# Latent-head scores from high and low parts in five passes, with the value projection moved ahead of the convolved queries and keys

## The chip, the cores and the metric

The kernel runs on one core of a Trainium2 chip. The metric is device time in microseconds (us) of one execution, taken as the median of several runs; less is better. The engines have short names in the rows: PE is TensorE (its weight loads are PEld), DVE is VectorE, ACT is ScalarE, POOL is GpSimd, SP is SyncE, which issues most DMA transfers.

## The reference, cut to what matters

Two transformer blocks over 512 tokens of width 1024, in float32. The change lies in the first block's mixer, which has two groups of heads over one normalised input h:

```python
z = h @ w_in[l]
q_m, k_m, v_m, o_m, gates, c_q, c_kv, k_pe = jnp.split(z, splits, axis=-1)
qk = jax.nn.silu(conv_centred(jnp.concatenate([q_m, k_m], axis=-1), conv_w[l], conv_b[l]))   # 5 taps over time
q_m, k_m = qk[..., :M_QK_W], qk[..., M_QK_W:]
y_a = mlstm_group(q_m, k_m, v_m, o_m, gates, ...)          # four recurrent heads, both directions
y_b = mla_group(c_q, c_kv, k_pe, cos, sin, ...)            # four latent heads
x = x + jnp.concatenate([y_a, y_b], axis=-1) @ w_out[l]
...
# mla_group: q and k of 4 heads, 128 plain + 64 rotated columns
s = jnp.einsum('bhqd,bhkd->bhqk', q_blk, kh) * scale       # 192 columns
p = jax.nn.softmax(s, axis=-1)
return jnp.einsum('bhqk,bhkv->bhqv', p, vh)
```

## The kernel before

A tensor is kept as 128 partitions by free columns. Two kinds of float32 matmul occur. One reads plain float32 operands; the trace lists each of these as two instructions. The other reads operands of type F32R that were split into a high part (a copy on ACT, rounded to F32R) and a low part (the difference, `sub`, on DVE), and `mm3` (lines 129 to 132) adds three passes, high by high, high by low and low by high. Weights come in pages of 128x1024 and are split the same way by `page` (line 105 on ACT, line 86 on DVE).

The order on each engine is fixed when the program is built, by a scheduler that looks at when operands and rooms (tiles in a pool, PSUM banks) come free; at run time each engine goes through its list in order and waits where it must. PSUM has four banks tagged "acc" and four tagged "att".

The stages that matter, with times in the profiled span:

- Projections and latent heads, 41 to 112.8 us. Line 426 and before prepare the compressed queries and keys. `lat_in`, `lat_norm` and `lat_heads` (lines 470 to 539) make, for 4 token blocks by 2 (query and key), the heads, normalise and rotate them, and transpose them: line 531 transposes the plain part, line 533 copies it to `qT0`/`kT0`; line 536 transposes the rotated part, line 537 copies it to `qT1`/`kT1`. All four are plain float32. Between these, PE works off two projections that nothing waits for yet: first `pq` (4 pages `wf[0..3]`, the queries and keys of the recurrent heads, 96 passes), then `pts` (the values, `w_in_t[0..3]`, 96 passes).
- The convolution of each `pq` page (lines 591 to 616): on DVE one line 596 and four lines 599 (the five taps) into `cv`, the tanh on ACT (line 602), line 603 on DVE, then copies on ACT (608, 610) and differences on DVE (line 86) into `qk` and `ql`.
- Attention of the latent heads, 112.8 to 174.9 us: 16 steps (4 heads by 4 query blocks), staged over three steps. `lat_scores` (lines 551 to 567): two plain float32 matmuls into `psc` (line 556 over 128 rows, line 557 over 64 rows), maximum on DVE (559, 560), exponential on ACT (563), reciprocal and scaling on DVE (564, 565). `lat_turn`: four transposes `ppt` (572) and a copy `PT` (574). `lat_out`: four matmuls `pov` (582), then `ybh` on ACT (583) and `ybl` on DVE (line 86, `yb`).
- Recurrent heads, 174.9 to 232 us: `pM` (641) brings the running maxima into an "acc" bank, `pS` (652, 653) the scores into an "att" bank, DVE and ACT build the weights `E` (664 to 668), `pH` (679) multiplies them with the values `v1`. From 194.7 us the projection of the output gate (`pts`, `w_in_t[4..7]`) fills PE between them.

The scores before:

```python
        PE.matmul(ps, qT0[j][:, jj, q], kT0[j][:, jj, :], start=True, stop=False)
        PE.matmul(ps, qT1[pp, j, q], kT1[pp, j, :], start=False, stop=True)
```

Of the kernel before, what the change touches and what calls it, by code (L numbers as in the profile page):

```python
# [7 lines left out]
F32 = mybir.dt.float32  # L8
F32R = mybir.dt.float32r
# [5 lines left out]
OP = mybir.AluOpType  # L15
# [35 lines left out]
def body(ctx, tc, I, out):  # L51
# [334 lines left out]
    zero = mb.tile([P, T], F32, tag="PT", name="zero", bufs=2)[0:R]  # L386
    G.memset(zero, 0.0)
    Bc = mb.tile([P, T], F32, tag="PT", name="Bc", bufs=2)[0:R]
# [20 lines left out]
    for i in range(3):  # L409
# [5 lines left out]
        ch = lp.tile([P, T], F32R, name=f"ch{i}")  # L415
        cl = lp.tile([P, T], F32R, name=f"cl{i}")
# [21 lines left out]
    qT0 = [main.tile([P, 2, T], F32, tag="x", name="qT0", bufs=NT) for _ in range(2)]  # L438
    kT0 = [main.tile([P, 2, T], F32, tag="x", name="kT0", bufs=NT) for _ in range(2)]
    qT1 = mb.tile([P, 2, T], F32, name="qT1")  # L440
    kT1 = mb.tile([P, 2, T], F32, name="kT1")
# [83 lines left out]
    def lat_heads(tb, key):  # L525
        nope, rot = lat[tb, key]
        T0, T1 = (kT0, kT1) if key else (qT0, qT1)
# [4 lines left out]
        for j in range(2):  # L532
            S.activation(T0[j][:, :, t], pt[:, j * 256:(j + 1) * 256].rearrange("p (h t) -> p h t", h=2), AF.Copy)
# [3 lines left out]
        S.activation(T1[:, :, t], pt[:, 0:256].rearrange("p (h t) -> p h t", h=2), AF.Copy)  # L537
# [13 lines left out]
    def lat_scores(hd, qb):  # L551
# [4 lines left out]
        PE.matmul(ps, qT0[j][:, jj, q], kT0[j][:, jj, :], start=True, stop=False)  # L556
        PE.matmul(ps, qT1[pp, j, q], kT1[pp, j, :], start=False, stop=True)
# [10 lines left out]
    def lat_turn(hd, qb):  # L568
        pe_ = att[hd, qb]
        pt = bank("att", "ppt")  # L570
        for sb in range(NT):
            PE.transpose(pt[:, sb * P:(sb + 1) * P], pe_[:, sb * P:(sb + 1) * P], ident)
        PT = mb.tile([P, NT, P], F32, tag="PT", name="PT", bufs=2)
        S.activation(PT, pt.rearrange("p (s t) -> p s t", s=NT), AF.Copy)
        att[hd, qb] = PT

# [13 lines left out]

    qk = []
    for i in range(4):
        ps = bank("acc", "pq")
        ws_mm(ps, page(wf[i]), h, l)
        cv = mc.tile([P, T], F32, tag="cv", name="cv", bufs=2)
        V.tensor_scalar(cv, ps, convw[:, i, 2:3], convw[:, i, 5:6], op0=OP.mult, op1=OP.add)
        for j in (0, 1, 3, 4):
            a, b = max(0, 2 - j), min(T, T + 2 - j)
            V.scalar_tensor_tensor(cv[:, a:b], ps[:, a + j - 2:b + j - 2], convw[:, i, j:j + 1], cv[:, a:b],
                                   op0=OP.mult, op1=OP.add)  # L600
        th = mc.tile([P, T], F32, tag="th", name="th", bufs=1)
        S.activation(th, cv, AF.Tanh, scale=0.5)
        V.scalar_tensor_tensor(th, th, 1.0, cv, op0=OP.add, op1=OP.mult)
        if i < 2:
            ql = mv.tile([P, T], F32R, name=f"ql{i}")
        for m, (own, other) in enumerate(((up, dn_), (dn_, up))):
            a = mv.tile([P, T], F32R, name=f"qk{i}{m}")
            S.activation(a[own], th[own], AF.Copy)
            if i < 2:
                S.activation(a[other], th[own], AF.Copy)  # L610
                sub(V, ql[own], th[own], a[own])
                qk.append((a, ql))
            else:
                sub(V, a[other], th[own], a[own])
                qk.append(a)


# [5 lines left out]

    def ev_o(tb, ps):
        S.activation(og[:, tb], ps, AF.Tanh, scale=0.5)
        V.scalar_tensor_tensor(og[:, tb], og[:, tb], 1.0, gm_b, op0=OP.add, op1=OP.mult)

    ts_mm([I["w_in_t"][j] for j in range(4)], range(KT), h, l, ev_v)
    mb_close()
    mc_close()  # L630


    ma, ma_close = pool("rec")
    og = ma.tile([P, NT, 512], F32, name="og")
    rec = {}
# [790 lines left out]
```

## Time and profile before

| | us |
|---|---|
| median of 3 runs (2143.5 to 2150.49) | 2144.11 |
| the profiled execution | 2146.64 |
| its span in the trace | 2144.8 |
| PE busy | 2096.8 (98%) |
| DVE busy | 1544.4 (72%) |
| ACT busy | 857.7 (40%) |

The profiled execution is 2.5 us above the median and lies inside the runs; 1.8 us of it are outside the span. A busy share is a mean over stages with different limits, so the rows below are taken stage by stage. A timeline row gives the start, the duration, the engine, the line, the operation, the tile written and the tiles read, the shape, the count of merged instructions, and in brackets the idle time of the engine before it and who ended that. Durations of neighbouring instructions overlap; the distance from one start to the next is what an instruction costs its engine.

### The profile page before, as it was taken

To read this page: it belongs to the slowest core of one execution; us is meant where nothing else is said; L and a number is where in the kernel's file an instruction comes from. 1 tells how busy PE (TensorE), PEld (TensorE's weight loads), DVE (VectorE), ACT (ScalarE), POOL (GpSimd) and SP (SyncE) were. 2 spreads that over 40 slices of the span, in tenths; PEclk is the share of its full clock that TensorE was granted. 3 is DMA by queue.
4 is the path that set the end of the run, shared out by engine and by line. 5 is a ranking of instruction groups with operands and counts; after the bars stand their busy time and mean duration, and the time that the engine had idled before them with its cause. 6 is when DMAs were issued, how large, how long until landed. Compare 5 with 4: busy or idle time off the path is not lost.

```text
span 2144.8 us, 29733 instructions
## 1 busy us (share of the span) xinstructions
PE 2096.8 (98%) x10985; PEld 1812.1 (84%) x10985; DVE 1544.4 (72%) x3037; ACT 857.7 (40%) x1504; POOL 504.0 (23%) x387
## 2 busy tenths in 40 slices
PE   8999999999999999999999999999999999999987
PEld 7856888888888778888999998888989989898976
DVE  6846675556454663689879697788888888888765
ACT  5745354444234543311345544333333333333323
POOL 1200034445100000100000002354444444444420
PEclk9999999999999999999999999999999999999999
DMA  5200279999422213345898857899999999999873
GB/s 199 69 30 20 89 256 343 324 347 345 170 68 89 70 61 102 124 163 178 284 364 301 280 187 242 286 360 362 342 349 338 335 336 349 337 345 341 280 234 108
DMA packets 178113, 504.40 MB, mean 235 GB/s; under 512 B 15536, under 2 KB 73776, under 8 KB 171184
## 3 DMA queue, kind: packets, MB, share of 16 engines
q1 hardware_dynamic: 135344, 326.33, 45.4%
q0 software_dynamic: 42624, 176.18, 21.9%
q8 instruction: 86, 1.41, 0.3%
q14 instruction: 59, 0.48, 0.1%
HBM read 426.95 MB, written 75.50 MB: 234 GB/s over the span
## 4 chain that ended last, share of the span: by engine, by line
PE 87%; DMA 5%; issue 3%; DVE 3%; ACT 1%; POOL 1%; SPq 0%; POOLq 0%; DVEq 0%; ACTq 0%
PE pA L130 10%; PE pA L131 10%; PE pA L132 10%; PE po L131 7%; PE po L132 7%; PE po L130 7%; PE pO L131 3%; PE pO L132 3%; PE pO L130 3%; PE pts L132 2%; PE pts L130 2%; PE pts L131 2%; PE pGm L1143 2%; DMA gv<-peer_v,eidx 2%; DMA gu<-peer_u_rows,eidx 1%
## 5 line engine op out<-in xcount | busy, mean ns | idle before, releaser
L130 PE MATMUL pA<-xTh,Ah 128*128 128x384 f32 (+1 forms) x1256 | 433.8, 345 | 0.3 <-ACT ge L1162 0.3
L132 PE MATMUL pA<-xTh,Al 128*128 128x384 f32 (+1 forms) x1256 | 434.1, 346 | 0.0
L131 PE MATMUL pA<-xTl,Ah 128*128 128x384 f32 (+1 forms) x1256 | 433.9, 345 | 0.0
L105 ACT ACTIVATE Ah<-raw 128x1024 fp32r<-128x1024 f32 x197 | 208.9, 1061 | 377.5 <-PE pA L131 266.7
L86 DVE TENSOR_TENSOR Al<-raw,Ah 128x1024 fp32r<-128x1024 f32 x196 | 242.8, 1239 | 144.1 <-ACT Ah L105 139.9
L1229 POOL DMA_INDIRECT gu<-peer_u_rows,eidx x128 | 172.6, 1348 | 607.2 <-ACT Wh L1286 404.8
L131 PE MATMUL po<-Bl,Wh 128*128 128x512 f32 x750 | 294.6, 393 | 14.1 <-DVE Bl L86 14.1
L132 PE MATMUL po<-Bh,Wl 128*128 128x512 f32 x750 | 294.3, 392 | 0.0
L130 PE MATMUL po<-Bh,Wh 128*128 128x512 f32 x750 | 281.5, 390 | 0.0
L131 PEld LDWEIGHTS pA<-xTl,Ah 128*128 128x128 f32 x1256 | 235.8, 188 | 13.2
L130 PEld LDWEIGHTS pA<-xTh,Ah 128*128 128x128 f32 x1256 | 235.8, 188 | 13.1 <-ACT ge L1162 0.6
L132 PEld LDWEIGHTS pA<-xTh,Al 128*128 128x128 f32 x1256 | 235.8, 188 | 9.3
L1240 POOL DMA_INDIRECT gv<-peer_v,eidx x128 | 169.6, 1325 | 222.6 <-DVE x L1242 202.4
L86 DVE TENSOR_TENSOR Bl<-raw,Bh 128x1024 fp32r<-128x1024 f32 x157 | 200.7, 1279 | 22.0 <-ACT Bh L105 21.7
L1286 ACT ACTIVATE Wh<-w 128x384 fp32r<-128x384 f32 x128 | 67.1, 525 | 319.7 <-PE po L131 316.4
L105 ACT ACTIVATE Bh<-raw 128x1024 fp32r<-128x1024 f32 x157 | 163.8, 1047 | 66.7 <-PE pO L132 46.2
L1231 DVE SCALAR_TENSOR_TENSOR gu<-gu,hn 128x1024 f32<-128x1024 f32 x128 | 156.0, 1219 | 34.3 <-DMA gu<-peer_u_rows,eidx 34.2
L131 PEld LDWEIGHTS po<-Bl,Wh 128*128 128x128 f32 x750 | 142.0, 189 | 42.7 <-DVE Bl L86 16.6
L1242 DVE SCALAR_TENSOR_TENSOR x<-gv,w,x 128x1024 f32<-128x1024 f32 x128 | 163.7, 1279 | 18.6 <-DMA gv<-peer_v,eidx 18.4
L132 PEld LDWEIGHTS po<-Bh,Wl 128*128 128x128 f32 x750 | 142.0, 189 | 29.5
L130 PEld LDWEIGHTS po<-Bh,Wh 128*128 128x128 f32 x750 | 141.2, 188 | 26.3
L86 POOL TENSOR_TENSOR shl<-sraw,shl 128x1024 fp32r<-128x1024 f32 x40 | 99.4, 2486 | 135.9 <-ACT shl L117 135.9
(409 smaller groups left out, 3679.4 us busy)
## 6 DMA issues: line engine op xcount, KB each, us to landing
raw<-peer_v SPq DMA_DIRECT2D x128, 512.0 KB
raw<-peer_u SPq DMA_DIRECT2D x104, 512.0 KB
Sd<-shl POOLq DMA_DIRECT2D x40, 1024.0 KB
raw<-w_ff SPq DMA_DIRECT2D x64, 512.0 KB
Gd<-stage SPq DMA_DIRECT2D x12, 2048.0 KB
Gt<-Gd SPq DMA_DIRECT2D x32, 768.0 KB
Al<-Sd SPq DMA_DIRECT2D x40, 512.0 KB
Ah<-Sd SPq DMA_DIRECT2D x40, 512.0 KB
```

What stands on the lines that cost most here:

```text
L86: eng.tensor_tensor(o, a, hi.bitcast(F32), op=OP.subtract)
L105: S.activation(hi, raw, AF.Copy)
L130: PE.matmul(ps, lh, rh, start=start, stop=False)
L131: PE.matmul(ps, lh, rl, start=False, stop=False)
L132: return PE.matmul(ps, ll, rh, start=False, stop=stop)
L1143: PE.matmul(o, hot[:, 0, jp, :, jb], val[:, p, jp, :, jb], start=p == 0, stop=p == 1)
L1229: G.indirect_dma_start(out=r, out_offset=None, in_=I["peer_u_rows"], in_offset=bass.IndirectOffsetOnAxis(ap=eidx[:, s:s + 1], axis=0))
L1231: V.scalar_tensor_tensor(r, r, 1.0, xn3, op0=OP.mult, op1=OP.mult, accum_out=act3[:, s:s + 1])
L1240: G.indirect_dma_start(out=r, out_offset=None, in_=I["peer_v"].rearrange("a p d -> (a p) d"), in_offset=bass.IndirectOffsetOnAxis(ap=eidx[ ...
L1242: V.scalar_tensor_tensor(x[3], r, w3[:, s:s + 1], x[3], op0=OP.mult, op1=OP.add)
L1286: S.activation(wh, w, AF.Copy)
```

## The change

Three things change together. The scores use high and low parts: `T0h`/`T0l` for the 128 plain rows (one `mm3`, three passes), and for the 64 rotated rows a tile `k1` that holds the high part in one half of the partitions and the low part in the other, against `q1`, which holds the query's high part in both halves (one pass over 128 rows), and one pass over 64 rows with the query's low part `q1l`. `lat_heads` makes these parts. The values now go ahead of the `pq` pages. And the convolution's tiles lie in the pool `rec`, which is opened after the latent heads' pools are closed, so that they share their room.

```diff
-    qT0 = [main.tile([P, 2, T], F32, tag="x", name="qT0", bufs=NT) for _ in range(2)]
-    kT0 = [main.tile([P, 2, T], F32, tag="x", name="kT0", bufs=NT) for _ in range(2)]
-    qT1 = mb.tile([P, 2, T], F32, name="qT1")
-    kT1 = mb.tile([P, 2, T], F32, name="kT1")
+    T0h = [[main.tile([P, 2, T], F32R, tag="x", name="T0h", bufs=NT) for _ in range(2)] for key in range(2)]
+    T0l = [mb.tile([P, 4, T], F32R, name=f"T0l{key}") for key in range(2)]
+    q1 = mb.tile([P, 4, T], F32R, tag="q1", name="q1", bufs=1)
+    q1l = main.tile([P, 2, T], F32R, tag="gb", name="q1l", bufs=1)
+    k1 = mb.tile([P, 4, T], F32R, name="k1")
...
         for j in range(2):
-            S.activation(T0[j][:, :, t], pt[:, j * 256:(j + 1) * 256].rearrange("p (h t) -> p h t", h=2), AF.Copy)
+            src = pt[:, j * 256:(j + 1) * 256].rearrange("p (h t) -> p h t", h=2)
+            S.activation(T0h[key][j][:, :, t], src, AF.Copy)
+            sub(V, T0l[key][:, 2 * j:2 * j + 2, t], src, T0h[key][j][:, :, t])
...
-        S.activation(T1[:, :, t], pt[:, 0:256].rearrange("p (h t) -> p h t", h=2), AF.Copy)
+        for m, (own, other) in enumerate(((up, dn_), (dn_, up))):
+            src = pt[own, 0:256].rearrange("p (h t) -> p h t", h=2)
+            T1 = (k1 if key else q1)[:, m::2, t]
+            S.activation(T1[own], src, AF.Copy)
+            if key:
+                sub(V, T1[other], src, T1[own])
+            else:
+                S.activation(T1[other], src, AF.Copy)
+                sub(V, q1l[own, :, t], src, T1[own])
...
-        PE.matmul(ps, qT0[j][:, jj, q], kT0[j][:, jj, :], start=True, stop=False)
-        PE.matmul(ps, qT1[pp, j, q], kT1[pp, j, :], start=False, stop=True)
+        (qh, kh), (ql, kl) = [T0h[key][j][:, jj] for key in range(2)], [T0l[key][:, hd] for key in range(2)]
+        mm3(ps, qh[:, q], ql[:, q], kh, kl, True, False)
+        PE.matmul(ps, q1[:, hd, q], k1[:, hd], start=False, stop=False)
+        PE.matmul(ps, q1l[pp, j, q], k1[pp, hd], start=False, stop=True)
...
-        PT = mb.tile([P, NT, P], F32, tag="PT", name="PT", bufs=2)
+        PT = lp.tile([P, NT, P], F32, tag="c", name="PT", bufs=6)
...
+    v1 = mv.tile([P, NT, 4, 129], F32, name="v1")
...
+    ts_mm([I["w_in_t"][j] for j in range(4)], range(KT), h, l, ev_v)
+    mb_close()
+    mc_close()
+    ma, ma_close = pool("rec")
+    qk = {}
+    for i in (0, 2, 1, 3):
         ps = bank("acc", "pq")
         ws_mm(ps, page(wf[i]), h, l)
-        cv = mc.tile([P, T], F32, tag="cv", name="cv", bufs=2)
+        cv = ma.tile([P, T], F32, tag=f"E{T}", name="cv", bufs=4)
...
-        th = mc.tile([P, T], F32, tag="th", name="th", bufs=1)
+        th = ma.tile([P, T], F32, tag=f"E{T}", name="th", bufs=4)
...
-    ts_mm([I["w_in_t"][j] for j in range(4)], range(KT), h, l, ev_v)
-    mb_close()
-    mc_close()
```

How this moves the instructions is seen at three places. The first is PE at the start of the attention; before, two steps' scores, then the steps in turn (`psc` scores, `ppt` transposes, `pov` values):

```order
L543 MATMUL pub<-ident,UB 128x128 x4
L556 MATMUL psc<-kT_532,qT_530 128x512 x2
L557 MATMUL psc<-kT_535,qT_534 128x512 x2
L572 MATMUL ppt<-ident,pe 128x128 x4
L556 MATMUL psc<-kT_532,qT_530 128x512
L557 MATMUL psc<-kT_535,qT_534 128x512
L572 MATMUL ppt<-ident,pe 128x128 x4
L582 MATMUL pov<-PT,vv 128x128 x4
```

And after, one such step (fourteen of the sixteen read like it):

```order
L130 MATMUL psc<-T0h 128x512
L131 MATMUL psc<-T0l_534,T0h 128x512
L132 MATMUL psc<-T0h,T0l_533 128x512
L569 MATMUL psc<-k_537,q_535 128x512
L570 MATMUL psc<-k_537,q1l 128x512
L585 MATMUL ppt<-ident,pe 128x128 x4
L595 MATMUL pov<-PT,vv 128x128 x4
```

In a step, two float32 matmuls have become five F32R passes; the transposes and the values stand as they stood.

The second place is DVE at the end of the attention. Before, the last `yb` differences are followed by the recurrent heads' work (`dd` and `E`); the four convolutions stand far ahead, among the latent heads' preparation:

```order
L565 TENSOR_SCALAR pe<-pe,sm 128x512
L86 TENSOR_TENSOR yb<-pov,yb 128x128 x2
L664 SCALAR_TENSOR_TENSOR dd<-pM,cols,cmask 128x128 x2
L86 TENSOR_TENSOR yb<-pov,yb 128x128
L668 SCALAR_TENSOR_TENSOR E<-pS,E 128x512
L664 SCALAR_TENSOR_TENSOR dd<-pM,cols,cmask 128x128
L668 SCALAR_TENSOR_TENSOR E<-pS,E 128x128
```

After, the first convolution starts between the last two of the sixteen `yb`; the other three and the next `E` follow:

```order
L578 TENSOR_SCALAR pe<-pe,sm 128x512
L86 TENSOR_TENSOR yb<-pov,yb 128x128 x2
L621 TENSOR_SCALAR cv<-pq,convw 128x512
L86 TENSOR_TENSOR yb<-pov,yb 128x128
L624 SCALAR_TENSOR_TENSOR cv<-pq,convw,cv 128x510
L624 SCALAR_TENSOR_TENSOR cv<-pq,convw,cv 128x511 x2
L624 SCALAR_TENSOR_TENSOR cv<-pq,convw,cv 128x510
L621 TENSOR_SCALAR cv<-pq,convw 128x512
L628 SCALAR_TENSOR_TENSOR th<-th,cv 128x512
L677 SCALAR_TENSOR_TENSOR dd<-pM,cols,cmask 128x128
```

From the first `cv` to the first `E` there are 4 rows of line 621, 16 of line 624, 4 of line 628, 6 differences, 2 `dd` and one `yb`; two more differences follow before the third `E`.

The third place is PE after the last `pov`. Before, the scores of the first recurrent head follow at once, `pM` of that head having run ahead of the attention:

```order
L582 MATMUL pov<-PT,vv 128x128 x8
L652 MATMUL pS<-qk_1397,qk_1494 128x512
L653 MATMUL pS<-ql_1396,qk_1494 128x512
L679 MATMUL pH<-v_1546,E 128x129 x3
L652 MATMUL pS<-qk_1401,qk_1497 128x512
```

After:

```order
L595 MATMUL pov<-PT,vv 128x128 x8
L654 MATMUL pM<-MxP,sel 128x512 x2
L665 MATMUL pS<-qk_1630,qk_1678 128x512
L666 MATMUL pS<-ql_1629,qk_1678 128x512
L654 MATMUL pM<-MxP,sel 128x512 x2
L692 MATMUL pH<-v_1454,E 128x129 x3
```

The first `pM` now stands behind the attention and needs a bank that a convolution has read, and `pS` needs the convolved query and key; in both programs the gate's projection comes only many rows later. From the end of the recurrent heads on, the lists of all engines read alike in both programs.

## Rows read from the trace of the kernel before

**Rows 1.** The chain that ended last, shares of the span by engine, from the page.

```profile
PE 87%; DMA 5%; issue 3%; DVE 3%; ACT 1%; POOL 1%; SPq 0%; POOLq 0%; DVEq 0%; ACTq 0%
```

**Rows 2.** Busy time of each engine by stretch; last columns granted clock, DMA share, GB/s.

```profile
50.00:108.00 58.00, 58.00 (x284) 48.90 (x283) 46.43 (x109) 40.64 (x109) 10.85 (x9) 1.00 0.24 73
...
128.90:174.90 46.00, 44.66 (x226) 26.19 (x225) 23.11 (x66) 20.72 (x54) 0.00 (x0) 1.00 0.13 46
174.90:194.70 19.80, 18.49 (x98) 12.39 (x96) 18.31 (x73) 15.55 (x56) 1.00 (x1) 1.00 0.01 2
```

**Rows 3.** Timeline of PE over one attention step (start, duration, engine, line, operation).

```profile
130.35 1.02 PE L556 MATMUL psc<-kT,qT 128*128 128x512 f32 x2
131.30 1.12 PE L557 MATMUL psc<-kT,qT 64*128 64x512 f32 x2
132.36 0.66 PE L572 MATMUL ppt<-ident,pe 128*128 128x128 f32 x4
...
133.74 1.02 PE L556 MATMUL psc<-kT,qT 128*128 128x512 f32 x2
```

**Rows 4.** Timeline of PE with F32R passes of 128 and of 64 rows.

```profile
199.12 0.40 PE L131 MATMUL pts<-Al,xTh 128*128 128x512 f32 x1
199.36 0.40 PE L652 MATMUL pS<-qk,qk 128*128 128x512 f32 x1
199.68 0.50 PE L653 MATMUL pS<-ql,qk 64*128 64x512 f32 x1
200.11 0.50 PE L132 MATMUL pts<-Ah,xTl 128*128 128x512 f32 x1
```

**Rows 5.** Timeline of PE at the last attention step.

```profile
169.68 0.66 PE L572 MATMUL ppt<-ident,pe 128*128 128x128 f32 x4
...
172.57 0.66 PE L572 MATMUL ppt<-ident,pe 128*128 128x128 f32 x4 [1.33 <-DVE pe L565]
```

**Rows 6.** Timeline of PE and windows around two stretches of half clock.

```profile
44.90:49.40 4.50, 4.50 (x19) 4.30 (x20) 4.46 (x10) 2.08 (x3) 0.00 (x0) 0.64 0.01 1
...
108.24 0.63 PE L641 MATMUL pM<-MxP,sel 128*128 128x512 f32 x2
...
112.82 1.97 PE L556 MATMUL psc<-kT,qT 128*128 128x512 f32 x4
...
118.60:128.00 9.40, 9.40 (x23) 4.89 (x24) 2.44 (x7) 2.23 (x5) 0.00 (x0) 0.50 0.00 0
```

**Rows 7.** DVE's groups of the convolutions (count, busy us, mean ns).

```profile
L599 DVE SCALAR_TENSOR_TENSOR cv<-pq,convw,cv 128x510 f32<-128x510 f32 x8 | 5.9, 742 | 0.1
...
L596 DVE TENSOR_SCALAR cv<-pq,convw 128x512 f32<-128x512 f32 x4 | 3.2, 806 | 0.4 <-PE pq L132 0.4
L603 DVE SCALAR_TENSOR_TENSOR th<-th,cv 128x512 f32<-128x512 f32 x4 | 2.7, 685 | 2.2 <-ACT th L602 2.2
L86 DVE TENSOR_TENSOR ql<-th,qk 64x512 fp32r<-64x512 f32 x4 | 2.7, 684 | 0.1
```

**Rows 8.** Timeline of DVE, a tap and the next tap that needs it.

```profile
55.00 0.81 DVE L596 TENSOR_SCALAR cv<-pq,convw 128x512 f32<-128x512 f32 x1 [0.40 <-PE pq L132]
55.84 0.75 DVE L599 SCALAR_TENSOR_TENSOR cv<-pq,convw,cv 128x510 f32<-128x510 f32 x1
```

**Rows 9.** ACT's groups of the same stretch.

```profile
L608 ACT ACTIVATE qk<-th 64x512 fp32r<-64x512 f32 x8 | 5.0, 631 | 2.6 <-DVE th L603 2.6
L602 ACT ACTIVATE th<-cv 128x512 f32<-128x512 f32 x4 | 2.6, 639 | 0.0
...
L533 ACT ACTIVATE qT<-pqt 128x256 f32<-128x256 f32 x4 | 1.5, 382 | 0.0
```

**Rows 10.** Timeline of DVE from the attention's end into the recurrent heads.

```profile
174.46 0.29 DVE L86 TENSOR_TENSOR yb<-pov,yb 128x128 fp32r<-128x128 f32 x1 [1.75 <-ACT yb L583]
...
176.42 0.69 DVE L668 SCALAR_TENSOR_TENSOR E<-pS,E 128x512 f32<-128x512 f32 x1 [0.45 <-ACT E L667]
...
178.11 0.56 DVE L668 SCALAR_TENSOR_TENSOR E<-pS,E 128x384 f32<-128x384 f32 x1 [0.28 <-ACT E L667]
```

More of the change, by code (lines that the diff above doesn't have):

```diff
@@ L385, in body @@
     V.scalar_tensor_tensor(zf, zf, 0.0, ea, op0=OP.min, op1=OP.subtract)
-    zero = mb.tile([P, T], F32, tag="PT", name="zero", bufs=2)[0:R]
+    zb = mb.tile([P, 4, T], F32, tag="q1", name="zb", bufs=1)
+    zero, Bc = zb[0:R, 0], zb[0:R, 1]
     G.memset(zero, 0.0)
-    Bc = mb.tile([P, T], F32, tag="PT", name="Bc", bufs=2)[0:R]
     G.memset(Bc, 0.0)
@@ L414, in body @@
             ws_mm(ps, page(wf[6]), h, l)
-        ch = lp.tile([P, T], F32R, name=f"ch{i}")
-        cl = lp.tile([P, T], F32R, name=f"cl{i}")
+        ch, cl = [lp.tile([P, T], F32R, tag="c", name=n, bufs=6) for n in ("ch", "cl")]
         S.activation(ch, ps, AF.Copy, scale=gcq[:, i:i + 1])
@@ L526, in lat_heads @@
         nope, rot = lat[tb, key]
-        T0, T1 = (kT0, kT1) if key else (qT0, qT1)
         t = slice(tb * P, (tb + 1) * P)
@@ L587, in body, with ev_v @@
     lp_close()
-    qk = []
-    for i in range(4):
+    v1 = mv.tile([P, NT, 4, 129], F32, name="v1")
+    G.memset(v1[:, :, :, 128:129], 1.0)
+    def ev_v(tb, ps):
+        S.activation(v1[:, tb, :, 0:128], ps.rearrange("p (h d) -> p h d", h=4), AF.Copy)
+    ts_mm([I["w_in_t"][j] for j in range(4)], range(KT), h, l, ev_v)
[4 more added lines that the diff above has]
+    for i in (0, 2, 1, 3):
         ps = bank("acc", "pq")
         ws_mm(ps, page(wf[i]), h, l)
-        cv = mc.tile([P, T], F32, tag="cv", name="cv", bufs=2)
+        cv = ma.tile([P, T], F32, tag=f"E{T}", name="cv", bufs=4)
         V.tensor_scalar(cv, ps, convw[:, i, 2:3], convw[:, i, 5:6], op0=OP.mult, op1=OP.add)
@@ L604, in body @@
         if i < 2:
-            ql = mv.tile([P, T], F32R, name=f"ql{i}")
+            ql = ma.tile([P, T], F32R, name=f"ql{i}")
         for m, (own, other) in enumerate(((up, dn_), (dn_, up))):
-            a = mv.tile([P, T], F32R, name=f"qk{i}{m}")
+            a = ma.tile([P, T], F32R, name=f"qk{i}{m}")
             S.activation(a[own], th[own], AF.Copy)
@@ L611, in body @@
                 sub(V, ql[own], th[own], a[own])
-                qk.append((a, ql))
+                qk[2 * i + m] = a, ql
             else:
                 sub(V, a[other], th[own], a[own])
-                qk.append(a)
-    v1 = mv.tile([P, NT, 4, 129], F32, name="v1")
-    G.memset(v1[:, :, :, 128:129], 1.0)
-    def ev_v(tb, ps):
-        S.activation(v1[:, tb, :, 0:128], ps.rearrange("p (h d) -> p h d", h=4), AF.Copy)
+                qk[2 * i + m] = a
+    og = ma.tile([P, NT, 512], F32, name="og")
+    rec = {}
     def ev_o(tb, ps):
```

3 lines of the change are left out of this document (removed).

## The prediction

> **What bounds the kernel now.** I read the chain of waits first: 87% of it is PE work [rows 1], so the time is the length of PE's list plus the places where PE stands still. Then the windows by stage [rows 2]: while the latent heads are prepared (50 to 108 us), PE is busy without a gap and DVE for 46.4 of 58 us, so the convolutions that DVE does there cost nothing now. In the attention PE is busy for 44.7 of 46 us, DVE for only 23.1. At the start of the recurrent heads (174.9 to 194.7) PE and DVE are both nearly full, 18.5 and 18.3 of 19.8 us. Then the timeline of one attention step [rows 3]: its period is 133.74 - 130.35 = 3.39 us, of which the scores take 132.36 - 130.35 = 2.01 and transposes and values 1.38. PE sets that period, but not by much: at the last step, where PE has nothing to put in between, the transposes come 172.57 - 169.68 = 2.89 us after the end of their scores [rows 5]. This is the softmax loop (maximum, exponential, scaling), and no step can be shorter. From 232 us on, the lists of all engines read alike in both programs, and PE carries the rest, so I let a shift at that point reach the end unchanged.
>
> **Part 1, the parts for the scores.** Per token block and side, ACT gets one or three more copies and DVE four differences, each over 256 columns; 16 copies and 32 differences in all. ACT's copy of that size is 0.38 us [rows 9], 6 us in sum, and the differences at the same price would be 12 us. In exchange the convolutions leave this stretch: on DVE 4 x 0.81, 16 x 0.74 (eight taps read 742, the other eight 740), 4 x 0.69 and 8 x 0.68 [rows 7], 23 us, and on ACT 4 x 0.64 and 12 x 0.63 [rows 9], 10 us. Both engines get lighter, and the cover, 192 projection passes on PE, is the same in number. So it costs nothing as long as PE has passes left. At the end it has none: from the last projection work (`pM` at 108.24) to the first scores (112.82) go 4.6 us now [rows 6]. After, this tail holds one page's split and about ten copies of at most 0.38 us one behind the other, again some 4 to 4.5 us. I take 0; bounds -1 (the four `pM` leave) to +2 (the copies don't overlap).
>
> **Part 2, the scores in five passes.** An F32R pass over 512 columns behind another takes 199.36 - 199.12 = 0.24 us, the pass ahead of one over 64 rows 0.32, the one over 64 rows 200.11 - 199.68 = 0.43 [rows 4]. With 0.32 for the first, which follows plain float32 work, the five take 0.32 + 0.24 + 0.24 + 0.32 + 0.43 = 1.55 us instead of 2.01. The step becomes 1.38 + 1.55 = 2.93 us, just above the loop's 2.89, a gain of 0.46. The bounds: 0.50 (the loop) and -0.14 (if every pass took 0.43).
>
> The first five scores are another matter, since there the granted clock is 0.50, the 1.2 GHz level, from 118.6 to 128 us, after PE had waited for the first softmax [rows 6]. Now from the first scores (112.82) to the end of the fifth (132.36) [rows 3] go 19.5 us. After: two scores at full clock 3.1; the loop's wait until 1.55 + 2.85 = 4.4; then at half clock transposes 0.9, scores 2.6, transposes 0.9, values 1.7, scores 2.6, together 8.7; then one step of 2.9 at full clock: 16.0. That gains 3.5. The eleven steps left gain 11 x 0.46 = 5.1. **Together -8.6** (bounds -11 to -5).
>
> The Trainium skill, page "TensorE: Matmul & The Clock Gate", section "Back-to-back issue gap", gives N/2.4 + 2.5 ns for a lone matmul and some 131 ns for N = 512 in a steady stream. As an estimate from that page, five passes would cost 1.08 or 0.66 us; the step would then be the loop's 2.89 us, and the sum 0.4 us lower. The trace's 0.24 us does not bear out the smaller figure.
>
> **Part 3, the convolutions behind the attention.** DVE works through its list in order, and the first `cv` now stands behind the fifteenth of sixteen `yb`, which ends now at 174.46 + 0.29 = 174.75 [rows 10]. From there to the first `E` (176.42) are 1.7 us now, to the third `E` (178.11) 3.4. After, all four convolutions lie between. Their instructions: 4 x 0.81 + 16 x 0.74 = 15.1, 4 x 0.69 = 2.7, six differences 6 x 0.68 = 4.1, two `dd` and one `yb` about 1.0, in sum 22.9 us of durations; neighbours overlap by some 0.07 us, 30 times, -2.1: 20.8. Where a tap needs the tap ahead of it, the distance is 55.84 - 55.00 = 0.84 instead of 0.67 to 0.74 [rows 8]: four in the first convolution and two later, about +0.75. The last tanh has no cover: 0.64 us [rows 9] and the handing over, +0.75. So 22.3 us to the first `E`, and with two more differences ahead of the third 24.8. **This part adds 24.8 - 3.4 = +21.4 us** (bounds +19, if the overlaps are larger, to +24, if ACT's copies come late).
>
> Who waits: behind `cv` on DVE stand `dd` and `E`; on PE, `pS` waits for the convolved query and key and `pH` for `E`. All four "acc" banks hold a `pq` until its convolution has read it, so neither `pM` nor the gate's projection (the only work that could fill PE) can start; in PE's list it stands behind seven `pS`. PE is idle for some 20 us. What was a cover before, the gapless PE of 50 to 108 us, is gone for this work.
>
> **Part 4, the clock after that gap.** The first `pH` starts after a long idle, so at half clock. Each of the two stretches of half clock [rows 6], 4.5 and 9.4 us long, follows a wait of PE for another engine; as long a one here adds 2.3 to 4.7 us of PE time. PE has about 1.3 us of slack against DVE there (19.8 less 18.5) [rows 2] and the gap has moved the third `E` later than the first `pH`, another 0.4 to 1. I take +1.2 (bounds 0 to +4).
>
> **The sum**: 0 - 8.6 + 21.4 + 1.2 = +14.0 us. On the profiled execution, 2146.6 + 14.0 = 2160.6; on the median, 2.5 us below it and inside the runs' spread, 2144.1 + 14.0 = **2158.1 us**. A change of 0.3%, 6.4 us, is about what a measurement of this kernel can tell from none.
>
> **The rivals.** (a) *The clock stays down.* After the gap PE's work up to 194.7 comes in pieces between waits for DVE, and the clock stays at 1.2 GHz for all of it: some 15 us of PE work cost 7.5 more, less the slack of 1.7, +5.8 instead of +1.2: 2144.1 + 18.6 = 2162.7. For it: from 118.6 us it took 9.4 us to come back. Against: in both stretches of [rows 6] it came back.
>
> The Trainium skill, page "TensorE: Matmul & The Clock Gate", section "Why this matters for your kernels", says that a PE which idles between bursts of matmuls goes back to half its clock and that the loop should keep matmuls back to back. By that rule the change is a bad trade whatever the five passes save, and this rival's time is the one it points to.
>
> (b) *The five passes don't shorten the step*, because the loop in a running step is longer than 2.89 us (PE, DVE and ACT meet in it): the eleven steps gain nothing, 2144.1 + 14.0 + 5.1 = 2163.2. Against: the loop's length was read with the copy `PT` in it.
>
> (c) *The convolutions hide behind the attention, and it gets faster.* DVE has 46.0 - 23.1 = 22.9 us free in it [rows 2], about what they need. If the first `cv` started there, only the gain of part 2 would be left, 2144.1 - 8.6 = 2135.5. It is decided by where `cv` stands in DVE's list: ahead of the first steps' softmax it would be this, behind the fifteenth `yb` it is not. The list says the latter, and an engine doesn't overtake itself.
>
> (d) *Part of the gap is given back.* The recurrent heads start with scores and two `dd` already done, and PE's waits before the feed-forward layers could shrink, since loads that don't wait for PE have longer to land: 3 to 7 us less, 2151 to 2155. Against: the lists are alike, and most loads wait for buffers that PE frees.
>
> **How the numbers follow.** The forecast (2155 to 2161) 0.62, (a) 0.13, (b) 0.06, (c) 0.03, (d) 0.16. For 8 in 10 the range reaches down into (d) and up over (a) and (b): 2152 to 2165. Slower by over 0.3% is above 2150.5: all but (c) and about a third of (d), 0.91; within 0.3% 0.06; faster 0.03.
>
> **What would show each step.** Part 1: the first `psc` within 112 to 115 us, PE gapless up to 108. Part 2: a period of 2.9 to 3.0 us in the attention, the last `pov` ending at about 166. Part 3: PE almost without work for 20 to 23 us behind it, its wait for the first `pH` put down to DVE's `E`, and DVE full. Part 4: a granted clock of about 0.5 in the first few us after the gap. The forecast is wrong if `cv` starts well before the last `pov`, if the step stays above 3.2 us, or if the shift of some 14 us at the end of the recurrent heads isn't there at the end of the span.

## The result, and the profile of the changed kernel

| | before | after |
|---|---|---|
| median of six runs each, us | 2145.4 | 2162.31 (2155.76 to 2163.52) |
| ratio to before, 95% interval | 1 | 1.007 (1.0056 to 1.0084) |
| profiled execution, its span, us | 2146.64, 2144.8 | 2163.19, 2161.4 |
| PE busy, us | 2096.8 | 2096.8 |

The change makes the kernel slower, by 15 us by the ratio (12 to 18) and by 17 by the medians. The forecast was 2158.1, +14.0, in a range of 2152 to 2165. PE is busy for as long as before, in a span 16.6 us longer: on balance, what came is waiting.

The chain of waits of after, which answers [rows 1]:

```profile
PE 88%; DMA 4%; issue 3%; DVE 3%; POOL 1%; ACT 1%; POOLq 0%; DVEq 0%; SPq 0%; ACTq 0%
```

It reads like before's, since shares of a whole span don't show 20 us. The windows by stage do (columns as in [rows 2]: PE, PEld, DVE, ACT, POOL, then the granted clock). The second row is the attention, from its first scores to the end of its last values; the third goes on to the first `pH`, the fourth to the gate's projection:

```profile
50.00:108.00 58.00, 58.00 (x281) 48.85 (x280) 35.57 (x102) 36.39 (x108) 9.31 (x10) 0.98 0.24 70
115.18:169.84 54.66, 51.11 (x274) 37.40 (x272) 27.70 (x81) 26.57 (x67) 0.00 (x0) 0.89 0.14 50
169.84:194.05 24.21, 8.93 (x12) 3.47 (x13) 22.88 (x37) 11.07 (x20) 0.00 (x0) 0.54 0.00 0
194.05:214.10 20.05, 18.27 (x88) 13.60 (x88) 18.13 (x72) 14.00 (x53) 1.01 (x1) 0.79 0.00 1
```

The third row is the new thing: for 24.21 us DVE is busy for 22.88 and PE for 8.93, most of that at half clock. In before the same stretch reads:

```profile
175.13:178.28 3.15, 3.15 (x8) 1.29 (x8) 2.38 (x8) 2.13 (x8) 0.00 (x0) 1.00 0.00 0
```

In the first row DVE has 35.57 us where it had 46.43: the convolutions have left the preparation. One attention step of after on PE, which answers [rows 3] and [rows 4]:

```profile
158.53 0.63 PE L585 MATMUL ppt<-ident,pe 128*128 128x128 f32 x4
158.99 1.06 PE L595 MATMUL pov<-PT,vv 128*128 128x128 f32 x8
159.80 0.48 PE L130 MATMUL psc<-T0h 128*128 128x512 f32 x1
160.12 0.39 PE L131 MATMUL psc<-T0l,T0h 128*128 128x512 f32 x1
160.35 0.40 PE L132 MATMUL psc<-T0h,T0l 128*128 128x512 f32 x1
160.58 0.39 PE L569 MATMUL psc<-k,q 128*128 128x512 f32 x1
160.90 0.49 PE L570 MATMUL psc<-k,q1l 64*128 64x512 f32 x1
...
164.42 0.63 PE L585 MATMUL ppt<-ident,pe 128*128 128x128 f32 x4
```

Two periods take 164.42 - 158.53 = 5.89 us, 2.94 each (3.39 before). Starts of the five passes lie 0.32, 0.23, 0.23 and 0.32 us apart; with the 0.43 of [rows 4] for the last the scores cost 1.53 us. Transposes and values cost 159.80 - 158.53 = 1.27 us. That is 2.80 us of work in a step of 2.94; over five such steps PE is busy for 14.63 of 15.00 us:

```profile
145.00:160.00 15.00, 14.63 (x89) 10.98 (x89) 8.32 (x25) 7.89 (x22) 0.00 (x0) 1.00 0.00 1
```

DVE behind the attention, which answers [rows 7, 8, 10] (the rows between, all of them convolution work or `dd`, are left out):

```profile
169.17 0.29 DVE L86 TENSOR_TENSOR yb<-pov,yb 128x128 fp32r<-128x128 f32 x1 [1.75 <-ACT yb L596]
169.87 0.81 DVE L621 TENSOR_SCALAR cv<-pq,convw 128x512 f32<-128x512 f32 x1 [0.41 <-PE pov L595]
170.60 0.28 DVE L86 TENSOR_TENSOR yb<-pov,yb 128x128 fp32r<-128x128 f32 x1
170.80 3.09 DVE L624 SCALAR_TENSOR_TENSOR cv<-pq,convw,cv 128x510 f32<-128x510 f32 x4
...
192.28 0.69 DVE L628 SCALAR_TENSOR_TENSOR th<-th,cv 128x512 f32<-128x512 f32 x1 [0.76 <-ACT th L627]
192.95 0.89 DVE L681 SCALAR_TENSOR_TENSOR E<-pS,E 128x512 f32<-128x512 f32 x2
...
195.83 0.56 DVE L681 SCALAR_TENSOR_TENSOR E<-pS,E 128x384 f32<-128x384 f32 x1
```

The first `cv` waits for the last `pov`, since it lies in the attention's room, and then everything runs one behind the other. PE in the same stretch, with what ended each wait in brackets:

```profile
173.94 0.79 PE L654 MATMUL pM<-MxP,sel 128*128 128x512 f32 x1 [4.11 <-DVE cv L624]
179.85 0.80 PE L654 MATMUL pM<-MxP,sel 128*128 128x512 f32 x1 [5.11 <-DVE cv L624]
182.96 0.76 PE L665 MATMUL pS<-qk,qk 128*128 128x512 f32 x1 [2.32 <-DVE qk L86]
...
194.05 1.20 PE L692 MATMUL pH<-v,E 128*128 128x129 f32 x4 [1.68 <-ACT qk L633]
197.03 0.80 PE L692 MATMUL pH<-v,E 128*128 128x129 f32 x2 [1.77 <-DVE E L681]
```

`pM` waits for a bank that the convolution still reads, `pS` for the convolved operands. The first `pH` is put down to a copy on ACT (line 633), but the weights `E` that it reads end at 192.95 + 0.89 = 193.84, 0.2 us ahead of it; the next `pH` is put down to `E`.

### The profile page after: what moved, and what is told of

It is laid out like the page before. It is cut to its first block, busy times and chain, and to the rows that moved or that the text cites. A ratio compares the mean times of both kernels' runs of the same rounds, so it can differ in the third digit from the quotient of the medians.

```text
span 2161.4 us, 29828 instructions
## 1 busy us (share of the span) xinstructions
PE 2096.8 (97%) x11001; PEld 1821.1 (84%) x11001; DVE 1556.6 (72%) x3069; ACT 864.7 (40%) x1520; POOL 498.1 (23%) x387
## 4 chain that ended last, share of the span: by engine, by line
PE 88%; DMA 4%; issue 3%; DVE 3%; POOL 1%; ACT 1%; POOLq 0%; DVEq 0%; SPq 0%; ACTq 0%
PE pA L130 10%; PE pA L131 10%; PE pA L132 10%; PE po L131 7%; PE po L132 7%; PE po L130 7%; PE pO L131 3%; PE pO L132 3%; PE pO L130 3%; DMA gv<-peer_v,eidx 3%; PE pts L130 2%; PE pts L132 2%; PE pts L131 2%; PE pGm L1156 2%; PE pQ L130 1%
```

## The experiments

All were read by three distances: the start of the first scores, the length of the attention, and the way from the end of its last values to the start of the output projection (`out_half`, `pts` from `yb`). The third agrees to 0.6 us between the two profiles of after, the first two differ by some 3 us each. A ratio is to runs of before taken beside the kernel, whose medians lay between 2143.3 and 2145.7 us.

| kernel | first scores | attention | from there to `out_half` | rest of the span | median | ratio to before |
|---|---|---|---|---|---|---|
| before | 112.8 | 62.3 | 56.8 | 1912.8 | 2145.4 | 1 |
| after | 115.2 | 54.7 | 80.7 | 1910.9 | 2162.3 | 1.0070 |
| after, second profile | 112.1 | 51.5 | 80.1 | 1916.7 | 2161.0 | 1.0070 |
| five passes alone | 118.1 | 52.1 | 57.1 | 1913.6 | 2143.1 | 0.9995 |
| old scores, late convolutions | 110.0 | 57.7 | 80.4 | 1914.1 | 2165.2 | 1.0100 |
| wait filled | 112.6 | 51.5 | 80.0 | 1912.9 | 2159.3 | 1.0070 |
| three taps of five | 113.3 | 51.6 | 74.7 | 1918.9 | 2161.3 | 1.0074 |
| convolutions early again | 112.3 | 60.2 | 57.1 | 1913.0 | 2146.8 | 1.0015 |
| ... spread over the steps | 113.2 | 63.4 | 57.1 | 1916.8 | 2151.9 | 1.0028 |
| ... early, deeper staging | 113.6 | 55.8 | 57.1 | 1914.2 | 2142.8 | 0.9994 |
| ... spread, deeper staging | 113.2 | 48.0 | 56.8 | 1915.1 | 2133.2 | 0.9955 |
| before, deeper staging | 111.1 | 54.7 | 57.1 | 1913.1 | 2141.1 | 0.9984 |

The rest of the span lies between 1910.9 and 1918.9 us whatever was changed ahead of it: one total doesn't tell less than some 8 us. The exchange of PE's two projections is not in the table, since there the gate's projection no longer stands between the recurrent heads and `out_half`.

### The five passes alone

The edit puts `T0h`, `T0l`, `q1`, `q1l`, `k1` and the five passes into the kernel before.

```diff
...
-    qT1 = mb.tile([P, 2, T], F32, name="qT1")
-    kT1 = mb.tile([P, 2, T], F32, name="kT1")
...
+    T0l = mb.tile([P, 2, T], F32R, name="T0l")
+    q1 = mb.tile([P, 2, T], F32R, tag="q1", name="q1", bufs=1)
...
+    k1 = mb.tile([P, 2, T], F32R, name="k1")
```

> The kernel before with one thing of the change alone: the scores in five passes. Order, conv place and the values stay as before; so that the parts fit into the room, the four heads' low parts and rotated parts share tiles, so those scores are of wrong values. Theory (the conv block costs the time, the five passes save some): the period of a step falls from 3.39 to about 2.94 us, and the time falls by what the attention gains, 5 to 8.6 us, less up to 2.4 us for the later first scores: 2137 to 2142 against 2145.4 of before. Rival one (the five passes are worth nothing by themselves, since with the convolutions still in the stage ahead DVE has no room for the differences): the first scores come 5 us or more later and the time is within 3 us of before. Rival two (the five passes cost time): above 2148.

Measured: 0.9995 (0.9983 to 1.0007), no difference. Windows of the preparation, of its last 10 us and of the attention, and PE's longest wait in that end:

```profile
50.00:108.00 58.00, 57.39 (x276) 47.69 (x276) 52.79 (x119) 43.79 (x111) 9.45 (x8) 1.00 0.24 77
108.00:118.14 10.14, 5.43 (x28) 3.89 (x27) 8.08 (x28) 7.88 (x27) 2.01 (x2) 0.75 0.08 32
118.14:170.24 52.10, 47.43 (x275) 35.15 (x273) 28.23 (x82) 25.62 (x67) 0.00 (x0) 0.98 0.14 51
...
116.12 1.09 PE L530 MATMUL pqt<-ident,na 128*128 128x128 f32 x4 [1.77 <-DVE na L509]
```

Rival one holds: with convolutions and differences both, DVE is busy for 52.8 of 58 us, the heads come late, and the first scores 5.3 us later than in before. The shorter attention pays that back and little more.

### The old scores with the late convolutions

The edit takes `lat_heads` and the two plain float32 matmuls of before into the changed kernel; order and pools stay.

> The changed kernel with the old scores: two plain float32 matmuls again, no high and low parts; the values stay ahead of the convolved queries and keys, and the convolutions stay behind the attention. Theory: a step takes 3.4 us again and the wait of PE behind the attention stays, about 24 us; the time is before plus the conv block and the clock behind it, 2145.4 + 23 to 27, so 2168 to 2172, some 5 to 9 above the changed kernel. Rival one (the rise comes from the five passes and their copies): within 3 us of before. Rival two (the shorter step only moves the wait, so it saves nothing): the same as the changed kernel, 2162.

Measured: 1.0100 (1.0081 to 1.0119), 21 us above before. The attention and the wait behind it:

```profile
109.97:167.67 57.70, 54.48 (x257) 30.31 (x255) 29.12 (x80) 26.72 (x67) 0.00 (x0) 1.00 0.14 46
167.67:191.89 24.22, 8.63 (x12) 3.36 (x13) 22.88 (x37) 11.08 (x20) 0.00 (x0) 0.60 0.00 0
```

The wait is the changed kernel's to 0.01 us, so it is not the five passes'. The theory's time is missed by 3 us at its lower end. In the two profiles the difference lies ahead of the wait: the granted clock is 1.00 throughout the attention, where before's profile had the half clock of [rows 6] in it, and at full clock the old scores need 57.7 us, not 62.3. Whether before's other executions have that half clock, no profile shows.

### The wait filled, and the changed kernel once more

```diff
+    fill(h[:, 0, 0:P], 16)
     qk = {}
     for i in (0, 2, 1, 3):
...
+        if i in (0, 2):
+            fill(a[:, 0:P], 16)
```

`fill` makes 16 passes of 512 columns into a bank that nothing reads.

> The changed kernel with 48 passes of 512 columns that nothing reads, in three lots of 16 on PE: one behind the last values of the attention, one behind the first convolution's keys or queries, one behind the second's. They fill some 11 us of PE's wait. Theory (the low clock behind the wait costs some): the granted clock stays higher up to 202 us, PE's scores and weights from 194 to 202 go at full clock, and the recurrent heads start 2 to 4 us earlier: 2158 to 2160 against 2162.3. Rival one (DVE sets the pace there, so the clock costs nothing): the clock is up but the time is within 1.5 us of the changed kernel. Rival two (the lots don't keep the clock up, and delay pM or the scores): clock still 0.50 and the time the same or up to 3 us more.

Measured: 2159.27, inside the theory's range, though the ratio is 1.0070 as for after, and a granted clock of 0.86 instead of 0.54 in the wait:

```profile
164.11:188.44 24.33, 18.59 (x61) 12.74 (x60) 22.79 (x37) 11.09 (x20) 0.00 (x0) 0.86 0.00 1
188.44:207.71 19.27, 17.50 (x89) 12.86 (x89) 18.12 (x72) 14.00 (x53) 1.01 (x1) 0.82 0.00 0
```

But nothing was gained where it should have been: the first `pH` comes 24.33 us behind the last values, not 24.21, and the gate's projection 43.6 against 44.3. What this profile is ahead, it had won earlier, in an attention of 51.5 us that the edit doesn't touch. So the changed kernel was profiled a second time:

> The changed kernel once more, unchanged, for a second profiled execution: which of the differences between the executions belong to the program and which to the execution. Belonging to the program, by the account so far: 24.2 us from the last values of the attention to the first weights pH and some 44 us to the gate's projection, within 0.7 us of the first profile; a period of 2.94 us. Belonging to the execution: the half clock at 46 to 51 us and from 114 to 127.5 us; without them the first scores come at about 112.6 instead of 115.2 and the attention takes 51.5 instead of 54.7 us, as in the run with the filled wait. Rival: the half clock at 114 to 127.5 is there again and the first scores come at 115 again, so that the run with the filled wait had something of its own.

Its ratio is 1.0070 again (1.0043 to 1.0097), and its windows are those of the filled run:

```profile
112.08:163.60 51.52, 47.93 (x272) 35.43 (x272) 27.68 (x81) 26.64 (x67) 0.00 (x0) 0.97 0.15 52
163.60:187.83 24.23, 8.93 (x13) 3.46 (x13) 22.88 (x37) 11.10 (x20) 0.00 (x0) 0.59 0.00 0
187.83:207.31 19.48, 17.70 (x88) 13.08 (x88) 18.14 (x72) 14.05 (x53) 1.01 (x1) 0.81 0.01 1
```

The end of the preparation on PE, first in the first profile of after, then in the second:

```profile
112.89 0.41 PE L539 MATMUL pqt<-ident,ro 128*128 128x128 f32 x2 [1.63 <-DVE k L86]
114.32 1.09 PE L554 MATMUL pub<-ident,UB 128*128 128x128 f32 x4 [1.03 <-DVE T0l L86]
115.18 0.79 PE L130 MATMUL psc<-T0h 128*128 128x512 f32 x1
```

```profile
109.78 0.41 PE L539 MATMUL pqt<-ident,ro 128*128 128x128 f32 x2 [1.63 <-DVE k L86]
111.22 0.63 PE L554 MATMUL pub<-ident,UB 128*128 128x128 f32 x4 [1.03 <-DVE T0l L86]
112.08 0.50 PE L130 MATMUL psc<-T0h 128*128 128x512 f32 x1 [0.23 <-DVE q1l L86]
```

The two long waits are the same to 0.01 us (the third row of the second, 0.23 us, has no like in the first, where PE was slower); a first pass of 0.79 us is the 1.2 GHz level, one of 0.50 the 2.4 GHz level. In the first profile the granted clock was 0.50 from 45.5 to 52.3 us; in the second it was 1.00 from 18 to 112 us. So the half clock there and from 114 to 127.5 us belongs to an execution, the 24.2 us behind the attention to the program, and the filled run's 3 us are no effect of the filling.

### Three taps of five

```diff
-        for j in (0, 1, 3, 4):
+        for j in (1, 3):
```

> The changed kernel with three of five taps of each convolution: the two outer taps are left out, so eight instructions of 0.74 us on DVE are missing and the queries and keys of the recurrent heads have other values. Theory (the convolutions are exposed one for one): the first weights pH come 5.5 to 6.5 us sooner behind the last values of the attention than the 24.2 us of the changed kernel, the projection of the gate likewise, and the time falls by about 6 us, to 2154 to 2158. Rival (PE or the low clock sets the start of the recurrent heads): the time falls by less than 2.5 us.

```profile
164.86:182.74 17.88, 8.64 (x12) 3.36 (x13) 16.99 (x29) 11.08 (x20) 0.00 (x0) 0.62 0.00 0
```

The wait is 17.88 instead of 24.2 us, and `out_half` starts 74.7 us behind the last values instead of 80.1 to 80.7. Eight instructions of 0.74 us are 5.9, and the wait is 6.3 shorter: the convolutions are exposed one for one. The total does not show it (2161.3; 1.0074, 1.0049 to 1.0099), and by the time alone the rival would have won: four runs give an interval of 11 us, and in this profile the rest of the span was the longest of all, 1918.9 us. Whether other values in the later layers had a part in that was not tried.

### PE's two projections exchanged

```diff
...
+    ts_mm([I["w_in_t"][4 + j] for j in range(4)], range(KT), h, l, ev_o)
     mb_close()
...
-    ts_mm([I["w_in_t"][4 + j] for j in range(4)], range(KT), h, l, ev_o)
```

> The changed kernel with PE's two projections exchanged: the output gate's projection goes with the values into the preparation (its result lies in two tiles that are free there), and the convolved queries' and keys' projection (96 passes) goes behind the attention, where the convolutions are. All convolutions are still behind the attention and DVE still works 22 us on them, but PE has its 96 passes beside them. Theory (what the change lost is PE's idle time beside the convolutions): PE has 23 us of work there and waits only some 6 us for the first weights E, so the time is 2139 to 2150. Rival (DVE's list behind the attention, 22 us of convolutions and some 38 us of recurrent heads, is the bound up to 232 us, whatever PE has to do): PE waits later instead, and the time stays above 2154.

Measured: 1.0058 (1.0035 to 1.0081). It doesn't answer its question, since the scheduler laid the `pq` passes into the first 20 us of the attention (328 matmuls in it, not 272) and left PE nothing for the wait:

```profile
119.52:181.91 62.39, 58.87 (x328) 44.72 (x326) 31.34 (x84) 28.60 (x69) 0.00 (x0) 1.00 0.24 76
181.91:206.25 24.34, 8.94 (x13) 3.47 (x13) 22.87 (x37) 11.07 (x20) 0.00 (x0) 0.57 0.00 0
```

Still the wait is 24.3 us: its length is DVE's list. Whether 96 passes beside it would hide it stays open.

### The convolutions early again, with the five passes

The pool `latp` lies at the other end of the memory, is closed before the attention, and its 20 KB hold the convolved queries and keys; `cv` and `th` lie in `conv` as before, `PT` in two tiles `hn`.

```diff
-    lp, lp_close = pool("latp")
+    lp, lp_close = pool("latp", side="right")
...
+    lp_close()
+    lq, lq_close = pool("latq", side="right")
...
-        PT = lp.tile([P, NT, P], F32, tag="c", name="PT", bufs=6)
+        PT = tmp.tile([P, NT, P], F32, tag="hn", name="PT", bufs=2)
...
-    mb_close()
-    mc_close()
-    ma, ma_close = pool("rec")
...
-        cv = ma.tile([P, T], F32, tag=f"E{T}", name="cv", bufs=4)
+        cv = mc.tile([P, T], F32, tag="cv", name="cv", bufs=2)
```

> The changed kernel with one thing undone without giving up the five passes: the convolutions no longer wait for the end of the attention. The pool of the preparation is closed before the attention and its room holds the convolved queries and keys; the convolution's own tiles lie where they lay before; PT takes two tiles that are free by then. Values still ahead. DVE's list then has most of the taps between the latent heads' operations and some 15 operations of the convolutions among the first two softmaxes. Theory (the place of the conv block decides): the wait of about 24 us behind the attention is gone, 3 to 7 us of it come back as a later start of the steps, so 2139 to 2148. Rival one (the clock or the order of values and queries costs it, not the place of the convolutions): above 2154. Rival two (all is hidden, no new wait): 2134 to 2138.

Measured: 1.0015 (1.0000 to 1.0030), 2146.82, in the upper part of the theory's range. The wait behind the attention is gone (57.1 us to `out_half`), and the values still go ahead of the queries, so the order of the two is not what makes that wait. But the attention takes 60.15 us, most of it for this reason:

```profile
124.18 0.79 PE L657 MATMUL pM<-MxP,sel 128*128 128x512 f32 x1 [7.20 <-DVE cv L624]
```

DVE has the convolutions' last operations among the first two softmaxes, and PE stands for 7.2 us. They come so late because the queries and keys go behind the values: the last `pq` pass starts at 105.71 us, in before at 76.57.

### Spread over the steps, and the staging deeper

Spread: 16 of the operations are queued on DVE behind the softmax of steps 2 to 12 (`behind(n)` is `tc.issue_after` on that softmax's last instruction).

```diff
+        with behind(tht):
             V.scalar_tensor_tensor(th, th, 1.0, cv, op0=OP.add, op1=OP.mult)
```

> The run in which the convolutions were put back into the preparation and the first steps, with one thing more: 16 of their operations on DVE (the four differences of each pair, three of the last products with the tanh, the last convolution) may come only behind the softmax of steps 2 to 12, one or two to a step. In that run the first transposes of the attention came 12.4 us after the first scores (5.8 in before) and the attention took 60.1 us, where the same five passes took 51.5 us in a run at full clock. Theory (DVE has 1.2 us to spare in each step of 2.94): the attention takes 52 to 55 us, the recurrent heads start right behind it, and the time is 5 to 9 us below that run: 2136 to 2142, below before. Rival (an operation of the convolution in a step lengthens the softmax loop by its 0.7 us, since no step can be shorter than the loop): 16 x 0.7 = 11 us come back, the period reads 3.4 to 3.7 us, and the time is 2146 to 2150.

Measured: 1.0028 (1.0012 to 1.0043), 2151.9: the rival's side, a little above it. The attention is 63.4 us, 11.9 more than 51.5, 0.74 for each of the 16. A step with such an operation, on PE:

```profile
153.01 0.49 PE L580 MATMUL psc<-k,q1l 64*128 64x512 f32 x1
155.02 0.63 PE L595 MATMUL ppt<-ident,pe 128*128 128x128 f32 x4 [1.52 <-DVE pe L588]
```

DVE is busy for 38.25 of these 63.4 us, so it is not its load: a step's transposes stand on PE right behind the next step's scores, and a softmax that comes later meets no slack there. So the staging was made one step deeper, in this kernel, in the one before it and in before:

```diff
-    staged([(hd, qb) for hd in range(4) for qb in range(NT)], lat_scores, lat_turn, lat_out)
+    staged([(hd, qb) for hd in range(4) for qb in range(NT)], lat_scores, lambda hd, qb: None, lat_turn, lat_out)
```

> The run with the convolutions back in the preparation and the first steps, and the attention staged one step deeper: the transposes of a step come behind the scores of the second step after it, not of the next. Theory (the softmax loop, which takes 2.9 us from the end of a step's scores to its transposes and has 0.1 us to spare, hands every delay on DVE over to PE; with one step more between, PE's own 2.93 us set the period): PE has a third score to do while DVE works off the convolutions' last operations, the attention takes 53 to 57 us instead of 60.1, and the time falls by 3 to 7 us, to 2140 to 2144, below before or level with it. Rival (the first steps wait for DVE's convolutions however deep they are staged, and the pools' three pe tiles hold the depth back): the attention takes 59 us or more and the time stays at 2146 or above.

> The run with 16 operations of the convolutions spread over steps 2 to 12, and the attention staged one step deeper. Without the depth every operation in a step came back as time (63.4 us of attention against 51.5 + 16 x 0.7 = 62.7). Theory (it is the loop's length, not DVE's load: 1.7 us of work in a step and 1 us of convolution are less than 2.93): the period falls from about 3.7 to 3.0 us, the attention takes 52 to 56 us, and the time falls by 8 to 11 us against that run, to 2138 to 2143. Rival (DVE's or ACT's load is the bound): the attention stays above 60 us and the time above 2148.

> The kernel before with the deeper staging alone, as the measure for the two others. In before PE's 3.39 us of work set the period and the loop (2.9 us) had 0.5 us to spare, so theory: no change in the running steps; only at the start PE gets a third score, 2 us, to do during its wait for the first softmax, and at the end it waits for one step's loop less or as long, so the time falls by 0 to 3 us, to 2142 to 2146. Rival (the loop already sets the pace in before): more than 4 us less.

Measured: 0.9994 (0.9983 to 1.0006), 0.9955 (0.9936 to 0.9973) and 0.9984 (0.9971 to 0.9997). The attention and its middle in the spread kernel, and its scores on PE:

```profile
113.21:161.23 48.02, 47.71 (x276) 35.85 (x274) 36.79 (x98) 34.70 (x81) 0.00 (x0) 0.98 0.16 55
...
130.00:150.00 20.00, 20.00 (x119) 14.87 (x117) 17.22 (x44) 15.42 (x35) 0.00 (x0) 1.00 0.16 53
```

```profile
139.72 0.48 PE L134 MATMUL psc<-T0h 128*128 128x512 f32 x1
...
142.54 0.48 PE L134 MATMUL psc<-T0h 128*128 128x512 f32 x1
```

PE has no gap, the period is 2.82 us, with DVE at 17.2 of 20 us and the convolutions in it: theory and sign hold, and the gain is larger than expected (48.0 us against 52 to 56), since PE is never late. This kernel computes what before computes and is faster than before and after, by 9.6 us against before (6 to 14). The depth alone gives before 3.4 us (0.6 to 6), a little over its theory, with a granted clock of 1.00 throughout the attention. The rest, some 6 us, is the difference of two noisy figures; it is what the five passes give with the convolutions spread over the steps.

With the depth, and without spreading, the attention takes 55.8 us, as that theory said, but its first transposes still come 12.1 us after the first scores (12.4 without the depth): the wait for the convolutions at the start stays. In the running steps the period falls from 2.95 to 2.83 us, and PE, which was busy for 19.47 of 20 us from 140 to 160 us, has no gap:

```profile
140.00:160.00 20.00, 20.00 (x122) 15.16 (x122) 11.56 (x35) 11.53 (x29) 0.00 (x0) 1.00 0.16 54
```

## Why the prediction was right, and where it was not

**The sign and the main mechanism** were right: `cv` stands behind the fifteenth `yb`, DVE is full, and PE waits for it. Three runs test this. With the old scores the wait is the same, with eight taps of 5.9 us less it is 6.3 us shorter, and with the convolutions early again it is gone. All four parts lie inside their bounds, but two of them for other reasons than forecast. The first scores came at 115.2 and 112.1 us, where 112 to 115 was said.

**Part 1** was forecast at 0 (-1 to +2). PE has no gap from 50 to 108 us, as said, and the tail from the last projection pass to the first scores is 5.4 us in both profiles (109.77 to 115.18, 106.66 to 112.08), where before had 4.6 and the forecast 4 to 4.5: +0.8. Two larger terms cancel in it. The old scores with the same order start at 110.0, 2.9 us sooner than in before, so that is what the convolutions' leaving and the new order save. These two profiles had the same half clock ahead of it, before in the first row, the old scores in the second:

```profile
46.20:49.50 3.30, 3.30 (x12) 3.01 (x11) 3.26 (x5) 0.78 (x2) 0.00 (x0) 0.50 0.00 0
46.20:49.50 3.30, 3.30 (x11) 2.93 (x10) 3.26 (x5) 0.63 (x1) 0.00 (x0) 0.50 0.00 0
```

The parts then delay the first scores by 2.1 us against the second profile of after, which had no half clock there, and by 5.2 against the first, which had 6.8 us of it; halfway, as an estimate at like clock, some 3.7. What the count of the tail lacks is PE's waits for DVE's differences (1.63 us for `k`, 1.03 for `T0l`): only ACT's copies were added up.

**Part 2** was forecast at -8.6. The step has the forecast length, 2.94 for 2.93 us, but by luck. The scores take 1.53 us (1.55 forecast), the transposes and values 1.27 and not 1.38, so PE's own work is 2.8 us, and a softmax loop of 2.94 sets the period: it is longer in a running step than the 2.89 of [rows 5], as rival (b) said. The two kernels that differ by the depth alone show this: with the same passes the period falls from 2.95 to 2.83 us once the loop has a step of slack. The sum is smaller than forecast: 3.5 of it came from the first five scores, with half clock on both sides. In the two first profiles the attention goes from 62.3 to 54.7 us, -7.7; at full clock, or nearly (1.00 and 0.97), from 57.7 to 51.5 us, -6.2. That the half clock is the execution's is shown for after; for before, which was profiled once, the old scores with late convolutions stand in. By the medians the five passes are worth 3 to 4 us here (old scores 2165.2, changed kernel 2161.0 and 2162.3), by the ratios 6, with intervals that overlap; not 8.6.

**Part 3** was forecast at +21.4 (19 to 24) up to the third `E`. That comes 195.83 - 169.46 = 26.4 us behind the fifteenth `yb`, before 3.4: +23.0. Of the 1.6 too little 0.4 are the wait of `cv` for the last `pov`, which the list shows and the sum left out; the rest is spread over the distances between the operations.

**Part 4** was forecast at +1.2 (0 to 4). To the first `pH` the wait is 24.2 - 3.15 = +21.1; from there to `out_half` the changed kernel takes 55.9 to 56.5 us and before 53.7, so 2.2 to 2.8 more. Filling the wait won back at most 0.8 of it. It shortened the half clock but did not remove it, so how much of the 2.2 to 2.8 is the clock and how much DVE's list is not separated. Parts 3 and 4 together are +23.3 to +23.8, forecast 22.6; counted from the third `E` as in the forecast, part 4 is only +0.3 to +0.8. The length of the half clock was misjudged: not 4.5 or 9.4 us but some 30 (172 to 202 us), most of it in the wait, where it costs little. And the stretch of 4.5 us in [rows 6] was at half clock for some 3.4 us of it, which is why its window reads 0.64.

**The sum.** Forecast +14.0; in the two profiles `out_half` starts 18.5 and 11.7 us later than in before's, on either side of it, and the medians say +17. At like clock the measured terms are +0.8, -6.2 and +23.3 to +23.8, about +18; the ratio says +15. The misses of 0.8 in part 1, 2.4 in part 2 and 1.6 in part 3 all made the forecast too low, part 4 made it too high by less than 1. The narrower forecast of 2155 to 2161 us was missed by 1.3, the range held.

**The rivals.** (a) gave 2162.7, next to the median, and its low clock is there: 0.50 from about 172 to 202 us. By the Trainium skill's rule on an idle PE ("TensorE: Matmul & The Clock Gate", "Why this matters for your kernels") this was to be expected, and the trace agrees: PE stood still for 4.11 us up to 173.94 and for 5.11 up to 179.85. But the price of 5.8 us is not there. It was meant for all of PE's work between the wait and the gate's projection, and the clock came back 8.4 us into those 20; from the first `pH` to `out_half` the whole loss is 2.2 to 2.8 us. In the wait itself PE has little to do (8.93 of 24.21 us), and with the clock at 0.86 there the first `pH` came no sooner. Nor does the price follow from its own words: 15 us of PE work at half clock cost about as much again, not 7.5 more (the passes of a score start 0.43 us apart at half clock, 0.23 at full). A number that fits is no proof of its mechanism. (b) is out as a time, since the step is 2.94 us and not 3.39, though its longer loop is there. (c) did not happen, and the experiments show why it would not have been free: without depth each operation in a step costs its time. With depth it is what the fastest kernel does. (d) was forecast at 3 to 7 us back; the profiles show no such pattern, the rest of the span is 1910.9 and 1916.7 us against 1912.8.

## What to carry to other kernels

Work that is moved off a stage because of its room takes its whole length with it if its new place has nothing beside it: look for room that comes free earlier (here a pool that is done before the stage) before moving the work later. An engine that is half idle could take more work here only once the loop through it had a step of slack; staging one step deeper turned 0.74 us per operation into none. When two bounds of a step lie 0.04 us apart, as PE's work and the softmax loop did in the forecast, ask what each would be in the new kernel. And read a part's gain from two profiles, or between landmarks, before crediting it: one execution here differed from the next by 6 us up to the end of the attention, with the same code.

## What was not expected of the hardware

The granted clock of the same instructions differs from one execution to the next. At 47 to 50 us it was 0.50 in the first profile of after and 1.00 in the second; behind the first scores it was 0.50 up to 127.5 us in one, and 1.00 from 120 us on in the other, after waits of PE that were equal to 0.01 us (1.63 and 1.03 us, above). Together with its start that moved the end of the attention from 169.84 to 163.60 us. The total goes with the clock: of 25 executions of before taken beside the last runs, the four with a mean granted clock of 0.995 or 0.996 took 2136.3 to 2142.7 us, the seven at 0.991 took 2144.1 to 2148.3, and the one at 0.990 took 2151.3. The first profile of after had the lowest mean clock of that kernel's six executions (0.983, the others 0.985 to 0.988). What decides the clock, no run here shows.
